# Splitting the first load of a batched matmul into two DMAs, one row per partition first

## The chip, the cores and the metric

The kernel runs on one core of a Trainium2 chip. The metric is the device time of one execution in microseconds (us); the median over the runs is quoted, with the range in brackets where it matters.

## The reference

```python
batch, m, k, n = 16, 512, 512, 512          # a: [16, k, m], b: [16, k, n], float32
return np.matmul(a.transpose(0, 2, 1), b).astype(np.float32)
```

33.55 MB are read and 16.78 MB are written.

## The kernel before

All transfers are issued from one queue (the sync engine). The first batch is loaded in DMAs of its own so that work can start early: four rows of k to a partition, which are 8 KB in one piece, and all 128 partitions together are 1 MB. Later loads take 2 MB at once (16 KB to a partition). VectorE casts to bf16, TensorE multiplies, ScalarE empties PSUM into a large output tile, and the outputs are stored at the end.

```python
in0_v = [x.rearrange("batch (p r) m -> batch p r m", r=RV) for x in (a, b)]     # RV = 4 rows of 2 KB
...
for j in range(2):                       # batch 0: a, then b
    nc.sync.dma_start(x_ts[j][:, 0:RV, :], in0_v[j][0]).then_inc(s_f[j], 16)
for j in range(2):                       # batch 1
    nc.sync.dma_start(x_ts[j][:, RV:R, :], in0_v[j][1]).then_inc(s_x[j], 16)
for n in range(2, 2 * pairs):            # the other 14 batches, two at a time
    if n >= NX:
        nc.sync.wait_ge(s_in, n - NX + 1)
    ...
    nc.sync.dma_start(x[:], src).then_inc(s_x[n % NX], 16)
...
nc.vector.wait_ge(s_x[j] if u else s_f[j], 16)      # before the cast of batch u
```

Of the kernel before, what the change touches and what calls it, by code (L numbers as in the profile page):

```python
# [8 lines left out]
def kernel(  # L9
# [6 lines left out]
    nc = tc.nc  # L16
# [13 lines left out]
    RV = R // V  # L30
    T = M // P
    H = T // 2
    pairs = batch // G
    in_v = [x.rearrange("(pair g) (q r) m -> pair (g q) r m", g=G, r=R) for x in (a, b)]


    in0_v = [x.rearrange("batch (p r) m -> batch p r m", r=RV) for x in (a, b)]
# [13 lines left out]
    x_ts = [pool.tile([P, R, M], f32, name=f"x{j}") for j in range(NX)]  # L51
# [6 lines left out]
    s_x = [tc.alloc_semaphore(f"s_x{j}") for j in range(NX)]  # L58

    s_f = [tc.alloc_semaphore(f"s_f{j}") for j in range(2)]  # L60
    s_o0, s_o = s_f
# [7 lines left out]

    with tc.tile_critical(no_gpsimd_drain=True):  # L70
        for j in range(2):
            nc.sync.dma_start(x_ts[j][:, 0:RV, :], in0_v[j][0]).then_inc(s_f[j], 16)  # L72
        for j in range(2):
            nc.sync.dma_start(x_ts[j][:, RV:R, :], in0_v[j][1]).then_inc(s_x[j], 16)  # L74
        for n in range(2, 2 * pairs):
# [18 lines left out]
        for u in range(G):  # L94
            if u:
                nc.vector.wait_ge(s_mm, H)
            for j, bf_ts in enumerate((abf_ts, bbf_ts)):
                nc.vector.wait_ge(s_x[j] if u else s_f[j], 16)
                nc.vector.tensor_copy(  # L99
                    out=bf_ts[0][:], in_=x_ts[j][:, u * RV:(u + 1) * RV, :]  # L100
                ).then_inc(s_cast, 1)
                if u == G - 1:
                    nc.vector.memset(dve_done[:, j:j + 1], 0.0).then_inc(s_in, 1)  # L103
# [63 lines left out]

        for i in range(pairs):
            if i == NO:
                nc.scalar.wait_ge(s_o0, 32)  # L170
            if i == 0:
                for g in range(G):
                    for h in range(H):
                        nc.scalar.wait_ge(s_mm, H * g + h + 1)
                        nc.scalar.copy(  # L175
                            out=o_ts[0][:, g, 2 * h:2 * h + 2, :], in_=ps_ts[0][h][:]
                        ).then_inc(s_ev[h], 1)
            for h in range(H if i else 0):
                for g in range(G):
                    nc.scalar.wait_ge(s_mm, G * H * i + G * h + g + 1)  # L180
                    ev = nc.scalar.copy(  # L181
                        out=o_ts[i % NO][:, g, 2 * h:2 * h + 2, :], in_=ps_ts[g][h][:]
                    )
                ev.then_inc(s_ev[h], 1)

            nc.scalar.memzero(act_done[:, i:i + 1]).then_inc(s_out, 1)  # L186


    with tc.tile_critical(sync_engine=mybir.EngineType.Pool, no_gpsimd_drain=True):
        nc.gpsimd.wait_ge(s_o0, 32)  # L190
        nc.gpsimd.wait_ge(s_o, 16 * ((NO + 1) // 2))
    tc.no_sync_barrier()
    nc.sync.dma_start(out_v[:, batch - G:batch], o_ts[(pairs - 1) % NO])
# [30 lines left out]
```

## Time and profile before

| | before |
|---|---|
| time | 123.18 us (123.15 to 123.31) |
| span of the profiled run | 121.4 us |
| DMA: busy share of 16 engines over the span | 97.7% |
| rate from 3 to 119 us | 430 GB/s |
| TensorE, VectorE, ScalarE busy | 51%, 31%, 27% |

The DMA engines are the full resource; the lines that show it stand in the prediction.

Each DMA counts its semaphore up sixteen times, and the trace records every one. We read them as one for each of the sixteen DMA engines; the trace doesn't name the engine.

### The profile page before, as it was taken

What the parts mean: (1) busy time and instruction counts of PE and PEld (TensorE: products, weight loads), DVE (VectorE), ACT (ScalarE), POOL (GpSimd) and SP (SyncE); (2) the same over time, 40 slices, a digit from 0 to 9 for tenths busy, and PEclk for the clock granted to TensorE, in tenths of its full rate; (3) what the DMA queues carried; (4) which work ended last, traced back from release to release, by engine and by line L of the source; (5) the groups of instructions that cost most, each with busy time, mean ns of one, the idle gap of its engine ahead of it and who ended that gap; (6) DMA issues with size and microseconds to landing.
All of it is one profiled execution on the core that took longest, in us unless ns stands there. A gap on an engine that the chain in (4) does not pass through costs nothing.

```text
span 121.4 us, 1204 instructions
## 1 busy us (share of the span) xinstructions
PE 61.7 (51%) x480; PEld 35.0 (29%) x480; DVE 38.1 (31%) x48; ACT 32.2 (27%) x41; POOL 0.2 (0%) x4
## 2 busy tenths in 40 slices
PE   0007829099379559959919979989800000000000
PEld 0002314066156225536515636655400000000000
DVE  0061160864284090484265347492000000000000
ACT  4000423302900920390560084190009200000000
POOL 0000000000000000000000000000000000000000
PEclk9999999999999967999995999999995555555555
DMA  2999999999999999999999999999999999999994
GB/s 57 424 432 429 467 432 432 432 432 432 432 432 432 432 432 427 432 432 416 432 427 427 432 432 402 432 427 427 429 429 432 429 429 432 421 424 429 429 424 208
DMA packets 4864, 50.33 MB, mean 415 GB/s; under 512 B 384, under 2 KB 384, under 8 KB 384
## 3 DMA queue, kind: packets, MB, share of 16 engines
q1 hardware_dynamic: 4864, 50.33, 97.7%
HBM read 33.55 MB, written 16.78 MB: 415 GB/s over the span
## 4 chain that ended last, share of the span: by engine, by line
DMA 63%; DVE 6%; issue 3%; ACT 2%; SPq 2%; ACTq 1%
DMA x<-in_b_dram 53%; DMA out_dram<-o 10%; DVE bbf L118 3%; DVE abf L118 3%; ACT o L181 2%; SPq L74 1%; ACTq L70 1%; SPq L72 1%; SPq L80 0%; DVE done L124 0%; ACT done L186 0%; SPq L219 0%; SPq L70 0%
## 5 line engine op out<-in xcount | busy, mean ns | idle before, releaser
L156 PE MATMUL ps<-bbf,abf 64*128 64x512 bf16 x448 | 53.0, 393 | 13.6 <-PEq L151 13.6
L156 PEld LDWEIGHTS ps<-bbf,abf 64*128 64x128 bf16 x448 | 31.3, 112 | 35.3 <-issue 20.6
L181 ACT COPY o<-ps 128x1024 f32<-128x1024 f32 x28 | 26.3, 1026 | 45.9 <-PE ps L156 37.0
L118 DVE CAST abf<-x 128x2048 bf16<-128x2048 f32 x14 | 17.1, 1224 | 17.5 <-PE ps L156 13.5
L118 DVE CAST bbf<-x 128x2048 bf16<-128x2048 f32 x14 | 17.1, 1225 | 14.6 <-DMA x<-in_b_dram 14.6
L136 PE MATMUL ps<-bbf,abf 128*128 128x512 bf16 x32 | 8.7, 433 | 12.4 <-PEq L134 12.4
L136 PEld LDWEIGHTS ps<-bbf,abf 128*128 128x128 bf16 x32 | 3.7, 121 | 16.9 <-issue 14.8
L175 ACT COPY o<-ps 128x1024 f32<-128x1024 f32 x4 | 4.0, 1012 | 15.9 <-PE ps L136 15.9
L99 DVE CAST abf<-x 128x2048 bf16<-128x2048 f32 x2 | 2.5, 1228 | 11.2 <-DMA x<-in_a_dram 5.8
L99 DVE CAST bbf<-x 128x2048 bf16<-128x2048 f32 x2 | 2.5, 1225 | 1.2 <-DMA x<-in_b_dram 1.2
L186 ACT ACTIVATE done<-done 1x1 uint32<-1x1 uint32 x8 | 1.6, 197 | 0.0
L175 ACT ACT_TABLE_LOAD x1 | 1.3, 1283 | 0.9 <-SPq L70 0.9
L124 DVE MEMSET done<- 1x1 f32 x14 | 0.8, 59 | 0.0
L103 DVE MEMSET done<- 1x1 f32 x2 | 0.1, 59 | 0.0
L208 POOL MEMSET const-bfloat16-1.0<- 128x1 bf16 x1 | 0.1, 102 | 0.0
L208 POOL MEMSET const-uint8-127<- 128x1 uint8 x1 | 0.1, 102 | 0.0
L208 POOL MEMSET const-float32-0.0<- 128x1 f32 x1 | 0.1, 99 | 0.2 <-issue 0.2
L208 POOL MEMSET const-float32-1.0<- 128x1 f32 x1 | 0.1, 99 | 0.0
## 6 DMA issues: line engine op xcount, KB each, us to landing
x<-in_a_dram SPq DMA_DIRECT2D x7, 2048.0 KB, 12.2
x<-in_b_dram SPq DMA_DIRECT2D x6, 2048.0 KB, 15.9
out_dram<-o SPq DMA_DIRECT2D x3, 4096.0 KB, 21.7
x<-in_b_dram SPq DMA_DIRECT2D x4, 1024.0 KB, 12.1
out_dram<-o SPq DMA_DIRECT2D x2, 2048.0 KB, 29.3
x<-in_a_dram SPq DMA_DIRECT2D x2, 1024.0 KB, 6.8
```

The lines of the kernel that those rows point to most:

```text
L70: with tc.tile_critical(no_gpsimd_drain=True):
L72: nc.sync.dma_start(x_ts[j][:, 0:RV, :], in0_v[j][0]).then_inc(s_f[j], 16)
L74: nc.sync.dma_start(x_ts[j][:, RV:R, :], in0_v[j][1]).then_inc(s_x[j], 16)
L99: nc.vector.tensor_copy(out=bf_ts[0][:], in_=x_ts[j][:, u * RV:(u + 1) * RV, :]).then_inc(s_cast, 1)
L118: nc.vector.tensor_copy(out=(bbf_ts if n % 2 else abf_ts)[v][:], in_=x_ts[n % NX][:, v * RV:(v + 1) * RV, :],).then_inc(s_cast, 1)
L124: nc.vector.memset(dve_done[:, n:n + 1], 0.0).then_inc(s_in, 1)
L136: mm = nc.tensor.matmul(ps_ts[0][h][:, t % 2, :], a_m[:, r, t], bbf_ts[0][:, r, :], start=(r == 0), stop=(r == RV - 1),)
L156: mm = nc.tensor.matmul(ps_ts[g][h][:, t % 2, :], a_m[:, t], bbf_ts[v][rows, r, :], start=(v == 0 and r == 0), stop=(v == V - 1 and r == R ...
L175: nc.scalar.copy(out=o_ts[0][:, g, 2 * h:2 * h + 2, :], in_=ps_ts[0][h][:]).then_inc(s_ev[h], 1)
L181: ev = nc.scalar.copy(out=o_ts[i % NO][:, g, 2 * h:2 * h + 2, :], in_=ps_ts[g][h][:])
L186: nc.scalar.memzero(act_done[:, i:i + 1]).then_inc(s_out, 1)
L208: nc = _bacc.Bacc("TRN2", target_bir_lowering=False, num_devices=1)
```

## The change

The intent is that the very first transfer is small, so that data may flow sooner. The first a comes in two DMAs over the same 128 partitions. The first takes one row of each partition, 2 KB out of every 8 KB; the second takes the other three, 6 KB out of every 8 KB.

```diff
         for j in range(2):
-            nc.sync.dma_start(x_ts[j][:, 0:RV, :], in0_v[j][0]).then_inc(s_f[j], 16)
+            cuts = (0, RV) if j else (0, 1, RV)
+            for r0, r1 in zip(cuts, cuts[1:]):
+                nc.sync.dma_start(
+                    x_ts[j][:, r0:r1, :], in0_v[j][0][:, r0:r1, :]
+                ).then_inc(s_f[j], 16)
...
-                nc.vector.wait_ge(s_x[j] if u else s_f[j], 16)
+                nc.vector.wait_ge(s_x[j] if u else s_f[j], 16 if u or j else 32)
...            # the first output's semaphore is the same one: 32 becomes 48 in two waits
```

More of the change, by code (lines that the diff above doesn't have):

```diff
@@ L169 @@
             if i == NO:
-                nc.scalar.wait_ge(s_o0, 32)
+                nc.scalar.wait_ge(s_o0, 48)
             if i == 0:
@@ L189 @@
     with tc.tile_critical(sync_engine=mybir.EngineType.Pool, no_gpsimd_drain=True):
-        nc.gpsimd.wait_ge(s_o0, 32)
+        nc.gpsimd.wait_ge(s_o0, 48)
         nc.gpsimd.wait_ge(s_o, 16 * ((NO + 1) // 2))
```

## The prediction

> **What bounds the kernel now.** I read the page first (busy shares, the sliced rows, the chain), then the page's table of DMA issues, then the busy time and DMA rate by stretch of time, then the timeline of the first 25 us and the queue's own waits. The page says which resource is full:
>
> ```profile
> PE 61.7 (51%) x480; PEld 35.0 (29%) x480; DVE 38.1 (31%) x48; ACT 32.2 (27%) x41; POOL 0.2 (0%) x4
> DMA  2999999999999999999999999999999999999994
> DMA packets 4864, 50.33 MB, mean 415 GB/s; under 512 B 384, under 2 KB 384, under 8 KB 384
> q1 hardware_dynamic: 4864, 50.33, 97.7%
> ```
>
> No compute engine is busy for much more than half of the span (121.4 us), while the 16 DMA engines are busy in every slice but the first and the last. The kernel is one stream of 50.33 MB through one queue. The stretches tell how steady it is (the last two columns are the DMA share and GB/s of packets that start in the stretch):
>
> ```profile
> 0.00:2.00 2.00, 0.00 (x0) 0.00 (x0) 0.00 (x0) 1.10 (x1) 0.20 (x4) 1.00 0.06 12
> 2.00:3.00 1.00, 0.00 (x0) 0.00 (x0) 0.00 (x0) 0.18 (x1) 0.00 (x0) 1.00 0.65 131
> 3.00:4.00 1.00, 0.00 (x0) 0.00 (x0) 0.00 (x0) 0.00 (x0) 0.00 (x0) 1.00 1.00 418
> ...
> 3.00:119.00 116.00, 61.65 (x480) 35.00 (x480) 38.07 (x48) 30.88 (x40) 0.00 (x0) 0.85 1.01 430
> ...
> 40.00:60.00 20.00, 16.20 (x136) 9.15 (x134) 9.47 (x12) 8.18 (x12) 0.00 (x0) 0.91 1.00 430
> 100.00:119.00 19.00, 0.00 (x0) 0.00 (x0) 0.00 (x0) 0.00 (x0) 0.00 (x0) 0.50 1.01 428
> 119.00:120.00 1.00, 0.00 (x0) 0.00 (x0) 0.00 (x0) 0.00 (x0) 0.00 (x0) 0.50 0.80 336
> ```
>
> From 3 to 119 us the stream runs at 430 GB/s with a share of 1: no hole. So the time is: when the stream starts, plus 50.33 MB / 430 GB/s = 117.05 us, plus what follows it. Only the first of these can be touched by this change. Where does the stream start? By 4.0 us, packets with 12 x 2 + 131 + 418 = 573 KB had started; at 430 GB/s these are 1.33 us, so it is as if full speed had begun at 4.0 - 1.33 = 2.67 us. Check: 2.67 + 117.05 = 119.7 us, and the last stretch's 336 KB are 0.78 us after 119. Finer stretches show the ramp:
>
> ```profile
> 0.90:1.90 1.00, 0.00 (x0) 0.00 (x0) 0.00 (x0) 1.00 (x1) 0.00 (x0) 1.00 0.00 0
> 1.90:2.20 0.30, 0.00 (x0) 0.00 (x0) 0.00 (x0) 0.28 (x1) 0.00 (x0) 1.00 1.09 164
> 2.20:2.60 0.40, 0.00 (x0) 0.00 (x0) 0.00 (x0) 0.00 (x0) 0.00 (x0) 1.00 0.49 82
> 2.60:2.90 0.30, 0.00 (x0) 0.00 (x0) 0.00 (x0) 0.00 (x0) 0.00 (x0) 1.00 0.73 218
> 2.90:3.20 0.30, 0.00 (x0) 0.00 (x0) 0.00 (x0) 0.00 (x0) 0.00 (x0) 1.00 0.99 410
> ```
>
> Multiply and divide by 8 KB: 6 packets start in 1.9 to 2.2, 4 in 2.2 to 2.6, 8 in 2.6 to 2.9. That is 18 packets for 16 engines in the first microsecond: about one first packet each, which in steady state takes 8192 B x 16 / 430 GB/s = 0.305 us. **The ramp costs about 2.67 - 2.0 = 0.7 us**, and the change works on nothing else.
>
> The issues that feed it, from the timeline:
>
> ```profile
> 0.94 0.39 SPq L72 DMA_DIRECT2D x<-in_a_dram  x1
> 1.39 0.42 SPq L72 DMA_DIRECT2D x<-in_b_dram  x1
> 1.86 0.42 SPq L74 DMA_DIRECT2D x<-in_a_dram  x1
> 2.33 0.66 SPq L74 DMA_DIRECT2D x<-in_b_dram  x1
> ...
> 16.10 0.33 SPq L80 DMA_DIRECT2D x<-in_a_dram  x1
> ```
>
> **What the Trainium skill says.** "DMA: Bandwidth & Descriptors", section "Why small descriptors are slow (HBM only)", gives a fixed cost of about 3 cycles per packet beside 32 B per cycle. Its fabric ceiling ("Specifications") is 435 GB/s at 850 MHz, so 3 cycles are an estimated 3.5 ns. The trace agrees: the stores (8 KB runs, 100 to 119 us) move 428 GB/s and the loads (16 KB packets, 40 to 60 us) 430; 131072/428 = 306.2 ns and 262144/430 = 609.6 ns leave 2 x 306.2 - 609.6 = 2.8 ns per packet, rough because the rates are rounded. "Perfetto Trace Analysis", section "DMA Optimizations", says that splitting helps where DMA engines are generally idle, and that transfers under 2 KB carry large overhead: here the engines are idle in the ramp alone, and the new runs are exactly 2 KB, not under. The same page, "Summary: the profiler window per engine type", says that the issue's window leaves out the movement of the data; the trace agrees, with the first issue over at 1.33 us and no packet before 1.9.
>
> **The change part by part.**
> - *Added: one issue on the sync queue.* 0.39 us plus the 0.06 us to the next start is 0.45 us. The first b issue slides from 1.39 to about 1.84, and the last of the six unblocked issues ends near 4.45 instead of 4.0. The stream has then moved (4.45 - 2.67) x 430 = 0.77 MB of the first 1.05 MB, so it doesn't run dry for the later issues.
> - *Added: a small first DMA.* 128 x 2 KB = 262 KB last 0.61 us at 430 GB/s. The other 786 KB are issued 0.45 us behind the first. By issue times the second part is there 0.16 us before the first is used up, so no hole in the plain count, but with little to spare.
> - *Added packets.* The tile had 128 packets of 8 KB and now has 128 of 2 KB and 128 of 6 KB, plus 16 completion packets of the new DMA (the page's 384 small ones are 24 issues x 16). Each engine gets 8 + 1 more: 9 x 2.8 ns = 0.03 us on the path.
> - *Moved: the wait for a.* VectorE waits for 32 instead of 16, that is for both halves. It starts the first cast at 5.78 us now; anything up to half a microsecond later is beside the path. The first issue that needs VectorE's release starts at 16.10, when two tiles are still queued whose cast begins at 22.82 only: over 6 us of backlog. The thresholds 32 to 48 of the first output's semaphore only count the extra 16.
> - *In the ramp.* Same number of first descriptors (128, eight per engine), each a quarter the size. If what holds the engines until 2.9 us is the arrival of descriptors or the first reads, and each engine gets one packet through in that time, it has moved 2 KB instead of 8 KB by then and has lost 6144 B x 16 / 430 = 0.23 us. If it is held by bytes, or several small packets get through at once, nothing is lost.
> Sum: +0.03 for packets, 0 to +0.23 in the ramp, nothing elsewhere. I take +0.07: 123.18 + 0.07 = **123.25 us**.
>
> **The rivals.**
> - *The ramp gets shorter.* Smaller first packets could pass while a large one is still waiting, so that data flow from 2.0 us. For it: the first 8 KB packets take far longer than 0.305 us (share 1.09 over 0.3 us with 6 packets in it is 1.09 x 0.3 x 16 / 6 = 0.87 us each). Against: the number of descriptors and the first issue stay, and no run says that size is what holds them. The most it can give is the whole ramp, 0.7 us (122.5); likely it gives 0.1 to 0.4 (122.8 to 123.1).
> - *A hole after the first part.* If the second DMA's packets need longer to get to an engine than the 0.45 us between issues, engines that have finished their eight 2 KB packets wait. For it: the ramp shows half of the engines (8 packets at 2.6 to 2.9) starting 0.65 us after the first six, longer than the 0.61 us of the first part, and the fourth issue takes 0.66 us, so something in the feeding is slow there. It would add up to an issue's 0.45 us: 123.4 to 123.65.
> - *The DMA no longer bounds the start, but a late b does.* The timeline has the first b cast at 8.19 us, and a later b delays the first matmuls; but 6 us of backlog stand between them and the stream, so this makes nothing of the time.
>
> **Range and chances.** No change beyond hundredths I give about one half; the loss of 0.2 to 0.45 us three tenths; a gain of 0.1 to 0.4 two tenths. Eight in ten lie in 122.90 to 123.65 us. Two per cent are 2.46 us. A gain is capped by the ramp at 0.7 us, so faster by 2% would need something outside this account (0.01), and slower by 2% a hole of five issues' length (0.01); within 2% has 0.98.
>
> **What would show the steps right or wrong.** The page should count 4864 + 128 + 16 = 5008 packets, of them 400 under 512 B and 400 + 128 + 128 = 656 under 8 KB. There should be three issues at the tile's line, with the b issue starting near 1.84. The stretch from 4 to 119 us must stay at 430 GB/s with a share of 1; the bytes started by 4.0 us tell the ramp: about 573 KB means no change, 100 KB fewer means 0.23 us lost. A dip in the stretches between 2.6 and 3.6 us would show the hole. VectorE's first cast of a should begin within 0.5 us of 5.78 and the time should not follow it. Wrong would be: a time under 122.9 with the ramp unchanged, a rate below 428 in the steady part, or any idle stretch of the DMA after 5 us.

## The result, and the profile after

The changed kernel took 124.18 us (124.07 to 124.59, 4 runs), against 123.19 us of the kernel before. The ratio is 1.0085, 95% interval 1.006 to 1.011. A ratio here is the mean time of one kernel's runs over that of the other's of the same rounds, so it is not quite the ratio of the quoted medians. The loss is within 2%, as the prediction had it, but 124.18 us lies outside the predicted 122.90 to 123.65.

The page of the kernel after, its DMA rows:

```profile
DMA packets 5008, 50.33 MB, mean 410 GB/s; under 512 B 400, under 2 KB 400, under 8 KB 656
q1 hardware_dynamic: 5008, 50.33, 96.6%
```

The packet counts are those that were predicted. The bytes are the same, and the share of the queue has fallen from 97.7% to 96.6%. The stretches tell where (last two columns: DMA share, GB/s of packets that start in it):

```profile
0.00:2.00 2.00, 0.00 (x0) 0.00 (x0) 0.00 (x0) 1.10 (x1) 0.20 (x4) 1.00 0.01 5
2.00:3.00 1.00, 0.00 (x0) 0.00 (x0) 0.00 (x0) 0.18 (x1) 0.00 (x0) 1.00 0.51 156
3.00:4.00 1.00, 0.00 (x0) 0.00 (x0) 0.00 (x0) 0.00 (x0) 0.00 (x0) 1.00 0.83 262
...
5.00:119.00 114.00, 62.38 (x480) 34.91 (x480) 37.89 (x48) 30.88 (x40) 0.00 (x0) 0.86 1.01 429
119.00:120.00 1.00, 0.00 (x0) 0.00 (x0) 0.00 (x0) 0.00 (x0) 0.00 (x0) 0.50 1.06 451
120.00:121.00 1.00, 0.00 (x0) 0.00 (x0) 0.00 (x0) 0.00 (x0) 0.00 (x0) 0.50 0.30 123
```

By 4.0 us packets with 5 x 2 + 156 + 262 = 428 KB have started, 145 KB fewer than the 573 KB before, which is 145/430 = 0.34 us. The steady part is untouched. At the end a new thing shows: from 120 to 121 us the DMA share is 0.30, where it was 0.00 before. The trace's increments for the last store go from 120.62 to 121.91 us, median 120.74, and the second last comes at 121.02. The median engine is 0.45 us later than before, and the last one 1.50 us. The last one decides; this profiled execution took 124.59 us, which is 1.50 more than the 123.09 us of the profiled one before. Its straggler is there from the beginning: the second part of a has landed by 6.21 us on fifteen engines and at 6.99 us on the last, and a lag of 0.6 to 1.0 us goes through the whole run.

Finer stretches of the start, first before and then after:

```profile
3.20:3.50 0.30, 0.00 (x0) 0.00 (x0) 0.00 (x0) 0.00 (x0) 0.00 (x0) 1.00 0.97 410
```

```profile
2.60:2.90 0.30, 0.00 (x0) 0.00 (x0) 0.00 (x0) 0.00 (x0) 0.00 (x0) 1.00 0.52 130
2.90:3.20 0.30, 0.00 (x0) 0.00 (x0) 0.00 (x0) 0.00 (x0) 0.00 (x0) 1.00 1.07 287
3.20:3.50 0.30, 0.00 (x0) 0.00 (x0) 0.00 (x0) 0.00 (x0) 0.00 (x0) 1.00 0.52 123
```

Part of the loss is thus time in which engines have no packet under way. Summed from the trace's packets, an engine stood empty for 0.19 us between 3 and 4 us, and for 0.18 and 0.17 us in two later profiles with the same split (after_again, after_late); before, it was nothing. At 3.3 us 11, 9 and 11 packets ran in these three profiles, though 27, 38 and 28 of the 2 KB packets of the first part hadn't started. Of the packets that ran, 6, 7 and 7 were 6 KB ones of the second part, and seven engines finish the first part by 3.60 us in each. So the engines that stood empty were most likely those that still had 2 KB packets to come, not those that waited for the second part.

The issues, from the timeline of the kernel after, stand where they were expected (start, us it took); b's is at 1.86:

```profile
0.94 0.87 SPq L75 DMA_DIRECT2D x<-in_a_dram  x2
1.86 0.42 SPq L75 DMA_DIRECT2D x<-in_b_dram  x1
...
7.01 1.23 DVE L104 CAST abf<-x 128x2048 bf16<-128x2048 f32 x1 [7.01 <-DMA x<-in_a_dram]
```

VectorE's first cast has slid from 5.78 to 7.01 us, because it waits for the slowest engine's share of a.

So two questions stand: why the median engine loses 0.45 us, and why the engines drift apart.

### The profile page after: what moved, and what is told of

The parts are those of the page before. It is cut to its first block, busy times and chain, and to the rows that moved or that the text cites. A ratio compares the mean times of both kernels' runs of the same rounds, so it can differ in the third digit from the quotient of the medians. Undisturbed runs are those within 1.5% of the kernel's fastest.

```text
span 122.8 us, 1205 instructions
## 1 busy us (share of the span) xinstructions
PE 62.4 (51%) x480; PEld 34.9 (28%) x480; DVE 37.9 (31%) x48; ACT 32.2 (26%) x41; POOL 0.2 (0%) x4
## 2 busy tenths in 40 slices
DMA packets 5008, 50.33 MB, mean 410 GB/s; under 512 B 400, under 2 KB 400, under 8 KB 656
## 3 DMA queue, kind: packets, MB, share of 16 engines
q1 hardware_dynamic: 5008, 50.33, 96.6%
## 4 chain that ended last, share of the span: by engine, by line
DMA 54%; DVE 5%; PE 5%; ACT 2%; issue 2%; ACTq 1%; DVEq 0%
DMA x<-in_b_dram 35%; DMA out_dram<-o 10%; DMA x<-in_a_dram 9%; PE ps L141 5%; ACT o L186 2%; DVE bbf L123 2%; DVE abf L123 2%; DVE abf L104 1%; ACTq L71 1%; DVE done L129 0%; ACT done L191 0%; DVE bbf L104 0%; DVEq L122 0%
## 5 line engine op out<-in xcount | busy, mean ns | idle before, releaser
L161 PE MATMUL ps<-bbf,abf 64*128 64x512 bf16 x448 | 51.3, 384 | 14.3 <-PEq L156 14.3
L141 PE MATMUL ps<-bbf,abf 128*128 128x512 bf16 x32 | 11.1, 522 | 13.7 <-PEq L139 13.7
```

What stands on the lines that cost most here:

```text
L141: mm = nc.tensor.matmul(ps_ts[0][h][:, t % 2, :], a_m[:, r, t], bbf_ts[0][:, r, :], start=(r == 0), stop=(r == RV - 1),)
L161: mm = nc.tensor.matmul(ps_ts[g][h][:, t % 2, :], a_m[:, t], bbf_ts[v][rows, r, :], start=(v == 0 and r == 0), stop=(v == V - 1 and r == R ...
```

## The experiments

"Holes" below means that a DMA reads only a part of each 8 or 16 KB piece of HBM that belongs to a partition, and skips the rest; the pitch is the distance between the starts of two runs. Spread means the time from the first to the last of the sixteen increments of one DMA. Each run's kernel before was timed on the same chip in the same rounds, and its median was 123.17 to 123.29 us in every set. The diffs show the lines that matter; the counts that are waited for were adjusted.

| kernel | time, us | before, us | ratio (95% interval) |
|---|---|---|---|
| after_again | 124.03 | 123.29 | 1.0085 (1.0049 to 1.0122) |
| rows3_1 | 124.37 | 123.29 | 1.0092 (1.0077 to 1.0106) |
| b_split | 124.53 | 123.29 | 1.0097 (1.0082 to 1.0111) |
| mid_split | 124.32 | 123.29 | 1.0082 (1.0069 to 1.0095) |
| probe_contig | 123.91 | 123.24 | 1.0055 (1.0038 to 1.0072) |
| probe_pitch8 | 125.13 | 123.24 | 1.0155 (1.0138 to 1.0172) |
| probe_pitch16 | 124.82 | 123.24 | 1.0122 (1.0105 to 1.0139) |
| mid_half | 123.25 | 123.24 | 1.0000 (0.9983 to 1.0017) |
| contig_1_3 | 123.37 | 123.17 | 1.0022 (1.0010 to 1.0034) |
| contig_3_1 | 124.26 | 123.17 | 1.0085 (1.0072 to 1.0098) |
| half_start | 123.95 | 123.17 | 1.0061 (1.0048 to 1.0074) |
| rows_apart | 123.89 | 123.17 | 1.0062 (1.0049 to 1.0075) |
| contig_3_1_late | 124.22 | 123.21 | 1.0077 (1.0057 to 1.0097) |
| contig_3_1_swap | 123.71 | 123.21 | 1.0044 (1.0027 to 1.0061) |
| after_late | 123.97 | 123.21 | 1.0072 (1.0050 to 1.0095) |
| probe_4k_pitch8 | 125.10 | 123.21 | 1.0148 (1.0131 to 1.0165) |
| contig_1_3_swap | 123.36 | 123.22 | 1.0009 (0.9991 to 1.0026) |
| b_from_act | 123.40 | 123.22 | 1.0012 (0.9998 to 1.0026) |

### First set: is it the start?

**after_again**: the changed kernel once more, no edit.

> The changed kernel itself, once more. Seen so far: 124.07 to 124.59 us over four runs, and in the profiled one (the slowest of the four) one of the 16 DMA engines delivers its share of each tile about 0.8 us after the second slowest (6.99 against 6.21 us for the first a, 121.91 against 121.02 us for the last store). If the straggler is part of the change, this profile has it again, with a lag of 0.5 us or more, and the time is 124.0 to 124.6 us. If it was an accident of one execution, the last stays within 0.2 us of the second last, as in the kernel before (5.76 against 5.65), and the time is near 123.6, what the 15 other engines lost.

It took 124.03 us (one of six runs 125.48). This profiled execution (123.95 us) has no single straggler, 121.27 against 121.22 us for the two last engines, but the spread of the last store is 1.02 us (120.25 to 121.27). The bytes that had started by 4.0 us are 428 KB again. So the lone straggler was a feature of one execution; the wide spread is not. The 123.6 us that was expected without a straggler was missed. The account of this execution closes: the median engine is 120.77 - 120.29 = 0.48 us later than before, the last is 0.50 us behind the median instead of 0.12, which together are 0.86 us, and 123.95 - 123.09 = 0.86.

**rows3_1**:

```diff
-            cuts = (0, RV) if j else (0, 1, RV)
+            cuts = (0, RV) if j else (0, 3, RV)
```

> The same two DMAs of a in the other order of size: rows one to three first (6 KB runs), then the last row (2 KB runs). Same packets, same issues, same runs of HBM. Theory A (the first DMA is too small, it runs dry or fills the slow start with packets of 2 KB): the loss goes nearly away, 123.2 to 123.5 us. Theory B (strided reads of part of each 8 KB row are slow wherever they are in the pair, or one more issue costs its slot): 124.0 us or more, like the changed kernel.

124.37 us: theory A falls. A large first part doesn't save the time.

**b_split**:

```diff
-            cuts = (0, RV) if j else (0, 1, RV)
+            cuts = (0, 1, RV) if j else (0, RV)
```

> The first a whole, the first b in two DMAs (2 KB runs, then 6 KB runs). The small DMA then stands behind 1 MB of queued data. Theory A (the start): 123.2 us, within 0.1 of before, 573 KB started by 4.0 us as before. Theory B (strided runs of 2 and 6 KB are slow to read, or a short DMA always costs): 123.7 to 124.5 us.

124.53 us, the most of the four, though by 4.0 us the 573 KB of the kernel before had started. The loss stands where b's 2 KB runs pass: a packet of theirs took 176 ns on average. b's 6 KB runs, with holes as well, all took 234 ns, their full speed in this trace.

**mid_split**: the kernel before, with the fifth load cut.

```diff
+            if n == 2:
+                for r0, r1 in ((0, 1), (1, R)):
+                    nc.sync.dma_start(x[:, r0:r1, :], src[:, r0:r1, :]).then_inc(s_x[n], 16)
```

> The first two DMAs whole; the fifth load (a of the second pair) split into its first row (2 KB runs) and its other seven (14 KB runs), deep in the queue. All theories that blame the start: 123.2 us, plus 0.03 us for 8 more data packets and one completion packet per engine. A cost of the extra issue or of small packets as such: 123.6 us or more.

124.32 us: the theories that blame the start alone fall. The start was as before, batch 1's b lands with a spread of 0.27 us, then the DMA of 2 KB runs lands with a spread of 1.19 us (13.56 to 14.75 us), and it stays above 1.0 us until the last store. Stretches of mid_split, while the short DMA passes, in a queue that is full:

```profile
12.00:12.50 0.50, 0.50 (x3) 0.15 (x1) 0.00 (x0) 0.00 (x0) 0.00 (x0) 1.00 0.97 410
12.50:13.00 0.50, 0.50 (x2) 0.15 (x1) 0.00 (x0) 0.00 (x0) 0.00 (x0) 1.00 0.87 324
13.00:13.50 0.50, 0.50 (x2) 0.15 (x1) 0.00 (x0) 0.15 (x1) 0.00 (x0) 1.00 1.21 361
13.50:14.00 0.50, 0.50 (x3) 0.18 (x2) 0.00 (x0) 0.50 (x1) 0.00 (x0) 1.00 0.98 352
14.00:14.50 0.50, 0.50 (x3) 0.23 (x2) 0.00 (x0) 0.37 (x1) 0.00 (x0) 1.00 0.98 406
14.50:15.00 0.50, 0.50 (x4) 0.23 (x2) 0.00 (x0) 0.00 (x0) 0.00 (x0) 1.00 1.00 430
```

The rate dips below 430 while the share stays near 1: here the engines are occupied and move less, unlike in the start of the changed kernel, where some stood empty. That leaves the extra issue, the short packets as such, or the addresses.

### Second set: issue, short packet or address?

A probe is one more DMA as the fifth in the queue, of 128 runs of 2 KB into a tile that nobody reads. Only its source differs.

```diff
+        nc.sync.dma_start(scratch[:], SOURCE).then_inc(s_p, 16)
         for n in range(2, 2 * pairs):
# probe_contig:   SOURCE = a[2, 0:128, :]              128 rows one behind the other
# probe_pitch8:   SOURCE = in0_v[0][2][:, 0, :]        one row out of four
# probe_pitch16:  SOURCE = in_v[0][1][:, 0, :]         one row out of eight
```

**probe_contig**:

> The kernel before with one DMA more, as the fifth in the queue: 256 KB that nobody uses, 128 runs of 2 KB which lie one behind the other in HBM. Its bytes alone cost 262144 B / 430 GB/s = 0.61 us (estimate from the steady rate). The split deep in the queue cost 1.0 us with no byte more, and widened the landing of one DMA over the 16 engines from 0.27 to 1.19 us. Theory C (the address pattern: 2 KB out of every 8 or 16 KB are slow to read): here all is contiguous, so 123.25 + 0.65 = 123.9 us and a spread that stays near 0.3 us. Theory D (short packets as such: an engine gets or reads ahead too few of them): 124.6 to 125.1 us and a spread of about 1 us.

**probe_pitch8**:

> The same unused DMA of 128 runs of 2 KB in the same place, but read at a pitch of 8 KB, the pattern of the changed kernel's first DMA. Theory C: 124.6 us or more and a spread near 1 us, while its contiguous twin stays at 123.9. Theory D: the same as its contiguous twin, 124.6 to 125.1.

**probe_pitch16**:

> The same at a pitch of 16 KB, the pattern of the split deep in the queue. Theory C: at least as slow as at 8 KB, since the runs are spread over half as many different places; 124.7 to 125.5 us. Theory D: as the contiguous twin.

The contiguous probe added 0.67 us, of which 0.61 are its bytes. The probe at 8 KB pitch added 1.89 us and the one at 16 KB 1.58 us. Same bytes, same packets, same place in the queue: 1.22 and 0.91 us are the price of the addresses. Theory D falls: it had the contiguous probe at 124.6 us or more. Theory C missed in one point: the pitch of 16 KB was to cost at least as much as that of 8 KB. Stretches of probe_contig, then of probe_pitch8:

```profile
12.50:13.00 0.50, 0.50 (x3) 0.12 (x2) 0.00 (x0) 0.00 (x0) 0.00 (x0) 1.00 0.93 356
13.00:13.50 0.50, 0.50 (x4) 0.29 (x3) 0.00 (x0) 0.30 (x1) 0.00 (x0) 1.00 1.62 672
```

```profile
12.50:13.00 0.50, 0.50 (x2) 0.15 (x1) 0.00 (x0) 0.00 (x0) 0.00 (x0) 1.00 0.76 172
13.00:13.50 0.50, 0.50 (x3) 0.23 (x2) 0.00 (x0) 0.20 (x1) 0.00 (x0) 1.00 0.99 127
13.50:14.00 0.50, 0.50 (x4) 0.26 (x3) 0.00 (x0) 0.50 (x1) 0.00 (x0) 1.00 0.97 115
14.00:14.50 0.50, 0.50 (x4) 0.29 (x3) 0.00 (x0) 0.31 (x1) 0.00 (x0) 1.00 1.65 520
```

(A stretch in which long packets start counts all their bytes, hence values over 430.) At 8 KB pitch the stream falls to 115 to 172 GB/s for 1.5 us. In the trace, all 128 contiguous packets took 84 ns; at 8 KB pitch they took 207 ns on average. The expected wide spread didn't come at 8 KB pitch, where all engines were slowed about alike (14.50 to 14.95 us); it came at 16 KB (13.61 to 14.77 us).

**mid_half**: mid_split with `((0, RV), (RV, R))`, two halves of 8 KB runs.

> The fifth load in two DMAs of 8 KB runs at a pitch of 16 KB: as many issues and completions as the split that cost 1.0 us, no 2 KB run. Theory C in its strong form (any partial read of a row is slow): 123.6 to 124.3 us and a wider spread. Theory C for 2 KB runs only, and theory D: 123.2 to 123.35 us, spread 0.3 us. If one more DMA of any kind costs 1 us: 124.2 us.

123.25 us, nothing lost. One more issue, its completions and its packets are free here, and so are holes when the runs are 8 KB out of every 16 KB.

### Third set: the change without its holes

The rows of batch 0 are dealt to the partitions so that each part is one piece of HBM. Any dealing gives the right product if a and b share it, so b is cut too.

```diff
+            for r0, r1 in zip(cuts, cuts[1:]):            # cuts = (0, 1, RV) or (0, 3, RV), for a and b
+                rows = (a, b)[j][0][P * r0:P * r1, :].rearrange("(p r) m -> p r m", r=r1 - r0)
+                nc.sync.dma_start(x_ts[j][:, r0:r1, :], rows).then_inc(s_f[j], 16)
```

**contig_1_3**, with cuts `(0, 1, RV)`:

> The change with the address pattern taken away: the rows of the first batch are dealt to the partitions so that both DMAs of a read HBM without holes (the first 128 rows, one to a partition, then the other 384, three to a partition); b has to be dealt the same way and so comes in two DMAs too, one more than in the changed kernel. Runs of 2 and 6 KB as in the change. Theory C (the holes between the 2 KB runs cost the time): 123.25 plus 2 x 9 packets per engine at about 3 ns, 0.06 us: 123.2 to 123.5 us, though b is split as well. A loss that comes from the small first DMA at the start: 123.6 to 124.5 us. A start that gains from small first packets, once they are read without holes: below 123.1 us.

123.37 us against 124.03 to 124.18 of the changed kernel: the sizes, the order and even one more split are there, other addresses are read, and most of the loss is gone. Stretches of contig_1_3 in the start:

```profile
0.00:2.00 2.00, 0.00 (x0) 0.00 (x0) 0.00 (x0) 1.10 (x1) 0.20 (x4) 1.00 0.06 3
2.00:3.00 1.00, 0.00 (x0) 0.00 (x0) 0.00 (x0) 0.18 (x1) 0.00 (x0) 1.00 0.89 240
3.00:4.00 1.00, 0.00 (x0) 0.00 (x0) 0.00 (x0) 0.00 (x0) 0.00 (x0) 1.00 1.03 373
```

That is 6 + 240 + 373 = 619 KB by 4.0 us, 46 KB more than before: in this one profile the small first DMA does the start no harm and it is 0.1 us shorter, which the time does not keep.

**contig_3_1**, with cuts `(0, 3, RV)`:

> The same with three rows to a partition first (6 KB runs) and the single rows second. Theory C: 123.2 to 123.5 us again, where the same order read with holes took 124.37. It also asks whether the size of the first packets moves the start: if it does, this and its twin differ by more than 0.15 us.

124.26 us. This contradicts the plain form of theory C. There are no holes, and its 2 KB packets run at full speed (85 ns on average), but two 6 KB packets in b's part took over 1.1 us, at 5.4 us, and the last store has a spread of 0.99 us. (The average of its 6 KB packets, 274 ns, tells nothing: the first packets are slow in all the traces that were read, and contig_1_3_swap below has 280 ns, with all packets over 0.7 us before 3 us, and no such loss. The kernel before has four first packets of 1.13 to 1.16 us.)

**half_start**: the changed kernel with `(0, 2, RV)`.

> The changed kernel with its cut in the middle: two rows of each partition, then the other two, runs of 4 KB at a pitch of 8 KB, both DMAs with holes. 8 KB out of 16 cost nothing (123.25), 2 KB out of 8 cost 1.2 us in the probe. If it is the share of the addresses that is read (a half each time), nothing or little: 123.2 to 123.5 us. If it is the length of the run below 8 KB: 123.6 to 124.5 us.

123.95 us: holes cost with 4 KB runs too, in the kernel's real place.

**rows_apart**: the kernel before with `rearrange("(r p) m -> p r m", p=P)` for batch 0.

> The kernel before with the first a and b dealt so that a partition's four rows lie 256 KB apart: each DMA still reads 1 MB without holes, but in 512 runs of 2 KB. Theory C (holes): 2 x 24 more packets per engine at about 3.5 ns (a contiguous 2 KB packet starts every 80 ns, a quarter of an 8 KB one is 76.5) make 0.17 us: 123.3 to 123.6 us. If 2 KB runs are slow at the start of the kernel even without holes: 124 us or more.

123.89 us, more than theory C allowed. By 4.0 us only 340 KB had started, (573 - 340)/430 = 0.54 us late; with the 0.17 us of its many packets this is 0.71, and 0.72 was measured. Each DMA is whole as a set of bytes, but a partition's four runs lie 256 KB apart, and the start is slow.

### Fourth set: a full queue, or the place?

**contig_3_1_late**, contig_3_1 with the diff below:

> The kernel read without holes in the order 6 KB runs, 2 KB runs took 124.26 us, which the theory of the holes had at 123.2 to 123.5. In its trace the last of the eight unblocked issues takes 1.23 us (0.45 in its twin), and two engines stand still for over a microsecond meanwhile. Theory F: too many descriptors are queued ahead at that moment, and issuing into a full queue holds engines up. Here the eighth issue waits until the first a has landed (about 5.3 us), with over 10 us of work still queued. Theory F: 123.2 to 123.5 us. If the stall has to do with the order or the addresses: 124.0 to 124.4 us as before.

```diff
         for n in range(2, 2 * pairs):
+            if n == 3:                                    # after_late: n == 2
+                nc.sync.wait_ge(s_f[0], 32)
```

124.22 us: the stalls are still there. Theory F, the full queue, falls for this kernel.

**after_late**, the changed kernel with the same wait at `n == 2`:

> The changed kernel with its sixth and seventh issues held back until the first a has landed (6.5 to 7 us). In its trace the sixth issue took 0.77 us. If the full queue (theory F) makes its loss: 123.2 to 123.5 us. If the holes between the 2 KB runs make it (theory C): 123.9 to 124.3 us, unchanged.

123.97 us: it falls for the changed kernel too.

**contig_3_1_swap**, contig_3_1 with the diff below:

> The same dealing of rows as in the 6 KB then 2 KB kernel without holes, with the issues swapped: the 2 KB runs first, now from the last 128 rows. If the order makes the difference (by theory F, because the short DMA leaves the queue early): 123.2 to 123.5 us. If it is where in HBM the parts lie: 124.0 to 124.4 us.

```diff
-            for r0, r1 in zip((0, 3, RV), (0, 3, RV)[1:]):
+            for r0, r1 in ((3, RV), (0, 3)):
```

123.71 us, half of the loss. It is in between, and neither answer alone.

**probe_4k_pitch8**, SOURCE = `in0_v[0][2][:, 0:2, :]`:

> The unused DMA as the fifth in the queue, with 128 runs of 4 KB at a pitch of 8 KB: 524288 B / 430 GB/s = 1.22 us for its bytes (estimate from the steady rate), so 124.5 us if half of each 8 KB is read at full speed. If the runs of 4 KB are slowed as those of 2 KB were (their packets took 207 ns instead of 84): 125.0 us or more.

125.10 us, 1.89 over the kernel before; 1.22 are its bytes, so 0.67 us are lost. Half of each 8 KB is not read at full speed.

**contig_1_3_swap**: contig_1_3 with `for r0, r1 in ((1, RV), (0, 1))`.

> The last cell of a two by two table of kernels that read without holes. The 6 KB runs from the upper 384 rows, 2 KB first: 123.37 us; from the lower 384 rows, 2 KB first: 123.71, 6 KB first: 124.26. Here: the upper 384 rows, 6 KB first. If the order alone makes the loss of a microsecond: 124.1 to 124.4 us. If it is the place in HBM: 123.3 to 123.6 us. In between: both have a part. If 6 KB first is no slower here, order has no effect of its own.

123.36 us. The four kernels without holes:

| 6 KB runs from | 2 KB first | 6 KB first |
|---|---|---|
| rows 128 to 511 | 123.37 | 123.36 |
| rows 0 to 383 | 123.71 | 124.26 |

Over the kernel before of their own rounds these are 0.20 and 0.14 us, then 0.50 and 1.09 us. With the 6 KB runs from the upper rows, order is nothing. From the lower rows there is a loss, and more of it with 6 KB first. The place in HBM matters, again an address; the 2 KB runs change place too, so the table doesn't say which of the two it is. Which addresses clash stays open.

**b_from_act**:

```diff
-            nc.sync.dma_start(x_ts[j][:, 0:RV, :], in0_v[j][0]).then_inc(s_f[j], 16)
+            (nc.scalar if j else nc.sync).dma_start(x_ts[j][:, 0:RV, :], in0_v[j][0]).then_inc(s_f[j], 16)
```

> A try at a version faster than both: the kernel before, with its first b issued from ScalarE's queue at the same moment as the first a from the sync queue, so that the engines have descriptors of two transfers in the slow start. Nothing is split. The start costs the kernel before about 0.8 us per engine (0.4 idle, 0.4 in slow first packets). If the start lacks descriptors, part of this comes back: 122.7 to 123.1 us. If the first reads are slow by themselves: 123.2 us. If the two streams disturb each other: 123.4 us or more.

123.40 us, not told apart from the kernel before and no gain (the interval reaches down to 0.9998). Whether the first reads are slow by themselves or the streams disturb each other, it doesn't tell. No version here beats the kernel before.

## Why the prediction was wrong

- **What bounds the kernel** was right: start plus bytes over rate plus tail, and the middle kept 429 GB/s. But it took sixteen engines for one. The landings show that the last to finish sets the end, and that engines which one DMA has slowed unevenly stay apart (1.48 us between first and last at 6.99 us, 1.29 us at the end). In after_again this is 0.38 of 0.86 us (0.50 - 0.12 us behind the median), and the prediction had no term for it.
- **The added issue** was right: b's issue at 1.86 (1.84 predicted). mid_half, one issue more deep in the queue, cost 0.01 us; contig_1_3, two more at the start, 0.20 us with all else that it changes.
- **The added packets** were right: 5008, 400 and 656, and a cost that is lost in the noise: the contiguous probe, with 9 more packets per engine, cost 0.06 us beyond its bytes. The 2.8 ns per packet were weaker support than the prediction says, since they compare stores with loads.
- **"Moved: the wait for a"** missed its size (7.01 us, not within 0.5 us of 5.78), for the same reason as the rest. That it is beside the path is not contradicted: the stream stays at 429 GB/s after it. The same goes for the rival of a late b, whose first cast slid from 8.19 to 9.46 us.
- **The step that failed** is "In the ramp", which allowed at most 0.23 us, with the "nothing elsewhere" of the sum. It priced a packet by its length, and asked only how many pass in the slow start. Cutting 8 KB into 2 and 6 KB also turned a transfer of one whole megabyte into two with holes. The runs showed in its place that the price depends on the addresses that a DMA reads. The change lost 0.99 us; its sizes and order at other addresses lose 0.20 us (contig_1_3). Deep in the queue, runs of 2 KB at a pitch of 8 KB cost 1.22 us more than the same runs without holes (probe_pitch8 against probe_contig). In the changed kernel the loss showed as 0.34 us of missing bytes by 4.0 us, and as drift. That such a loss is a matter of the slow start alone, as the step had it, is refuted by mid_split, which lost 1.03 us with the start as before.
- **The rival of a hole after the first part** had its dip: the DMA share is 0.52 from 3.2 to 3.5 us. Its size fell short (123.65 us at most), and its reason doesn't fit: the empty engines most likely still had 2 KB packets of the first part to come, and contig_1_3, with the same sizes of a's parts and its second part issued as soon after the first, has no such dip (1.03 from 3 to 4 us). The rival of a shorter start is supported at most for contig_1_3, by 0.1 us in one profile.
- **The chances**: within 2% at 0.98 held. But none of the three sizes that shared the chances (hundredths, a loss of 0.2 to 0.45 us, a gain) took in a loss of 0.99 us.

What is shown: the tried patterns with holes slow 2 and 4 KB runs; the changed kernel's sizes and order with other addresses lose 0.2 us instead of 0.7 to 1.0 (after_again 0.74, the first runs 0.99). What is not: how the loss divides between its two DMAs (in b_split the 6 KB part ran at full speed in a full queue), why the addresses show as long packets in the probe but partly as empty engines in the start, why some engines fall behind others, and why the kernels with 6 KB runs without holes from the lower rows lose. "Holes" is thus one harmful pattern, not the whole rule.

## What to carry to other kernels

In a kernel bound by its DMA stream, a cut also changes the addresses that are read together, and a small DMA with holes can cost more than its own bytes (1.28 us over the 0.61 us of the probe at 8 KB pitch). Parts that are each one whole piece of HBM are worth a try, but no guarantee: here they lost from 0.14 us, which is within the noise, to 1.09 us, by their place. Runs of 8 KB with holes were free in the one place that was tried. Try such a cut deep in the queue as well as at the start: if it loses there too, the start alone is not the cause. Look at the sixteen landings of a DMA, not at its last alone, since most of a drift between the engines, once made, is carried to the end (1.19 us became 1.06 in mid_split, 1.64 became 0.99 in contig_3_1).

## What the Trainium skill lacked or had wrong

- "DMA: Bandwidth & Descriptors", section "Latency and other measured facts", lists row pitches from 512 KiB (207 GB/s, near the 214 that it calls full) to 8 MiB (103 GB/s), under large powers of two. Here a pitch of 8 KB with 2 KB runs fell to 115 to 172 GB/s against 430, and 4 KB runs at that pitch lost 0.67 us on 1.22 us of bytes. The page lists no pitch as small as these.
- "Perfetto Trace Analysis", section "DMA Optimizations", goes by size alone, with overhead below 2 KB. In these runs 2 KB packets took 84 ns when read without holes (the same place in the queue, 207 ns at 8 KB pitch), so at one size the addresses decided.
- No page that was read tells that the sixteen engines keep a drift: a spread of 1.19 us made at 14 us was still over 1.0 us at the last store (mid_split), and the time ends with the last engine.
- No page that was read explains why the kernel without holes lost 1.09 us with 6 KB runs from rows 0 to 383 (contig_3_1) and 0.14 us with those from rows 128 to 511 (contig_1_3_swap).
